# Three weight casts moved from ScalarE to VectorE, and GpSimd's decay broadcasts and key products given an order, in a two-layer hybrid encoder

## The chip, the cores and the metric

The kernel runs on one core of a Trainium2 chip. The metric is the device time of one execution in microseconds; the median of several is compared. The engines are PE (TensorE), DVE (VectorE), ACT (ScalarE), POOL (GpSimd) and SP (SyncE, which here only issues DMAs). Each works through its own instructions in order and waits on semaphores for the others.

## The reference

Two pre-norm layers on a sequence of 256 positions and width 1024, all in float32. Each layer projects the normalised input once, feeds a chunked gated DeltaNet (forward and backward) and a differential softmax attention, projects both branches, merges them with sigmoid gates and projects the result. Cut to what matters here:

```python
def chunk_gated_delta(q, k, v, g, beta):            # chunks of 64 positions, 8 heads
    g = jnp.cumsum(g.reshape(bsz, nh, nc, CHUNK), axis=-1)
    gdiff = g[..., :, None] - g[..., None, :]
    decay = jnp.where(lower, jnp.exp(jnp.where(lower, gdiff, 0.0)), 0.0)
    L = jnp.where(strict, jnp.einsum('bhncd,bhnmd->bhncm', kb, k) * decay, 0.0)
    T = lax.linalg.triangular_solve(eye + L, ..., lower=True, unit_diagonal=True)
    ...
    state = (state * jnp.exp(g_last)[..., None, None]
             + jnp.einsum('bhcd,bhce->bhde', k_c * jnp.exp(g_last[..., None] - g_c)[..., None], v_new))
...
for l in range(DEPTH):                               # DEPTH = 2
    h = rmsnorm(x, norm_w[l]); proj = h @ w_in[l]
    o_a = gated_delta_branch(...)                    # q, k, v, z of the first branch: qa, ka, va, za
    o_b = diff_attention_branch(...)                 # q, k, v, z of the second: qb, kb, vb, zb
    x = x + (sigmoid(ga) * (o_a @ w_pa[l]) + sigmoid(gb) * (o_b @ w_pb[l])) @ w_out[l]
```

The kernel uses chunks of 128 positions, two per sequence.

## The kernel before, in words

**Weights.** Every projection runs over four pairs of 128 input channels. A pair's float32 weights (`raw`, 128 partitions x 1024, 512 KB) come by a DMA on SP's queue into one of three buffers. ACT makes the rounded high part (`hi`, L230, a CAST), DVE the rest (`lo` = `raw` - `hi`, L232), and PE multiplies hi by hi, lo by hi and hi by lo. Names carry the projection, the layer and the group, and the pair: `hi_q{l}13` is pair 3 of the second q group of layer l. `proj_fm` (L298 to L302, `pf_q`) serves the convolved q, k and v, `proj_tm` (L244 to L246, `pp_qk` and others) the attention's q and k and the gates.

**Decays.** `decays(g, c)` handles four heads g of a chunk c: a DMA on POOL's queue broadcasts their cumulated log decays into `B` (L618), POOL adds for the factor of k (`kds`, L621) and masks with `affine_select` (L624), ACT takes eight Exps per call, 32 in all (L628). `weigh_k` subtracts and multiplies on DVE (`dsum` L634, `A` L635) with the gram products `kk` of PE (L611).

**The triangular solve.** `turn_blocks` takes the 32x32 blocks of `A` through memory (`adr`) into `la` and `lt`, DVE solves them in 31 steps (`X`, L670 and L671), and `spread_blocks` copies X transposed into `lt` (L674) and sends both to memory (`udr`, L678, four DMAs on POOL's queue). From there come `T` (L705, group 0 on POOL's queue, group 1 on SP's) and `U` (L709, SP). PE merges blocks with them (`y64p` L723, `zt` L737), and ACT copies y between (L727). Next on SP's queue behind U stand the weights of the gate projection, `raw_gb`. The attention heads (`sc`, maxima `mx`, Exp `es`, transposes `at`, `aT`, products `av`, and squares `sqj` of the output) run in between.

**Products of k.** `chunks` multiplies k by its factor on POOL (`ktm`, L795, four operations) and uses the result much later, in the state's matmuls `sp`.

**What sets the order.** The code is written as steps; a scheduler with a time line of its own sorts the instructions, and the program that it gives is fixed. `behind(ins)` (`tc.issue_after`) is an edge of order for that scheduler; it becomes a wait on the chip only where data ask for one. `mark` is a dictionary of instructions to point at.

Of the kernel before, what the change touches and what calls it, by code (L numbers as in the profile page):

```python
# [11 lines left out]
AF = mybir.ActivationFunctionType  # L12
# [37 lines left out]
def hybrid_encoder(  # L50
# [47 lines left out]
    def last(ap, n):  # L98
        return ap.unsqueeze(ap.ndim).to_broadcast(list(ap.shape) + [n])
# [104 lines left out]
    def behind(ins):  # L204
        return nullcontext() if ins is None else tc.issue_after(ins)

    def weights(w, c0, n, nm, homes=(None,) * 4, ahead=True, later=None, spare=(), held=None):

        for kp in range(4):
            act, dve = (later or {}).get(kp, (None, None))
            with tc.high_priority(offset=HP) if ahead and homes[kp] is None else nullcontext():
                if homes[kp] is not None:
                    hi, lo = homes[kp][:, 0], homes[kp][:, 1]
                else:
                    hi = wpool.tile([P, 2, 512], F32R, tag="hi", name=f"hi_{nm}{kp}", bufs=2)
                    lo = wpool.tile([P, 2, 512], F32R, tag="lo", name=f"lo_{nm}{kp}", bufs=2)
                if kp in spare:  # L220
                    raw = work.tile([P, 2, 512], F32, tag="w4a", name=f"raw_{nm}{kp}", bufs=2)
                else:
                    raw = wpool.tile([P, 2, 512], F32, tag="raw", name=f"raw_{nm}{kp}", bufs=3)
                load = (held or {}).get(kp)
                with behind(load):
                    (nc.scalar if load else nc.sync).dma_start(
                        out=raw[:, :, :n],
                        in_=w[kp * 256 : (kp + 1) * 256, c0 : c0 + n].rearrange("(k p) c -> p k c", p=P))
                with behind(act):
                    high = S.copy(hi[:, :, :n], raw[:, :, :n]).ins  # L230
                with behind(dve):
                    mark[nm, kp] = high, V.tensor_tensor(lo[:, :, :n], raw[:, :, :n],  # L232
                                                         hi[:, :, :n].bitcast(F32), ALU.subtract).ins
            for k in range(2):
                yield 2 * kp + k, hi[:, k, :n], lo[:, k, :n]

    def proj_tm(act, w, c0, n, evac, nm, places=(None,) * 4, spare=(), later=None):

        accs = banks2(f"pp_{nm}")
        for kt, hi, lo in weights(w, c0, n, nm, places, later=later, spare=spare):  # L240
            for m in range(NM):
                ts_ = slice(m * P, (m + 1) * P)
                o = accs[m][:, :n]
                T.matmul(o, act[kt // 4][:, 0, kt % 4, ts_], hi, start=kt == 0, stop=False)  # L244
                T.matmul(o, act[kt // 4][:, 0, kt % 4, ts_], lo, start=False, stop=False)  # L245
                mark["proj"] = T.matmul(o, act[kt // 4][:, 1, kt % 4, ts_], hi, start=False,  # L246
                                        stop=kt == KT - 1).ins
                mark["done", kt] = mark["proj"]
        for m in range(NM):
            evac(m, accs[m][:, :n])  # L250
# [33 lines left out]
            evac(m, o)  # L284
            yield

    def proj_fm(act, w, c0, evac, nm):


        accs = [a.rearrange("p (b t) -> p b t", b=2) for a in banks2(f"pf_{nm}")]  # L290
        for kt, hi, lo in weights(w, c0, 512, nm, later=mark.pop("later", None)):
            for b in range(4):
                cs = slice(b * P, (b + 1) * P)
                o = accs[b // 2][:, b % 2, :]
                first = kt == 0 and b % 2 == 0
                done = kt == KT - 1 and b % 2 == 1
                with behind(mark.pop("first", None)):
                    T.matmul(o, hi[:, cs], act[kt // 4][:, 0, kt % 4, :], start=first, stop=False,  # L298
                             skip_group_check=True)
# [41 lines left out]
    for l in range(DEPTH):  # L341
# [98 lines left out]
        def qk_part(s_, i):  # L440
                def evac_qk(m, ps):
                    st = work.tile([P, 512], F32, tag="w2a", name=f"stg{l}{s_}{i}{m}", bufs=2)
                    S.copy(st, ps)
                    g_ = st.rearrange("p (g e) -> p g e", e=DH)
                    x12 = g_[:, :, 0 : 2 * RD].rearrange("p g (x r) -> p g x r", x=2)
                    both = lambda t_: mid(mid(t_[:, m, :], 2), 8)
                    r4 = small.tile([P, 2, 8, 2, RD], F32, tag="r4", name=f"r4{l}{s_}{i}{m}", bufs=1)
                    V.tensor_tensor(r4[:, 0], x12, both(cos), ALU.mult)
                    V.tensor_tensor(r4[:, 1], x12, both(sin), ALU.mult)
                    V.tensor_tensor(x12[:, :, 0], r4[:, 0, :, 0], r4[:, 1, :, 1], ALU.subtract)  # L450
                    V.tensor_tensor(x12[:, :, 1], r4[:, 0, :, 1], r4[:, 1, :, 0], ALU.add)
# [64 lines left out]
        def conv(seg, c_base, slot, g):  # L516
            def evac_conv(acc, b0):
# [35 lines left out]
                for b in range(2):  # L553
                    for m in range(NM):
                        hd = 4 * g + b0 + b
                        S.activation(sqj[:, :P], ptv[:, b, m, :], AF.Square,
                                     accum_out=ss[:, m, hd : hd + 1])
            proj_fm(hT, wl, c_base + 512 * g, evac_conv, f"{seg}{l}{g}")

        gdr = dram.tile([NM, 8, 2, P], F32, tag="gdr", name=f"gdr{l}")  # L560
        lnc = small.tile([P, 2, NM, NH], F32, tag="lnc", name=f"lnc{l}")
# [50 lines left out]
                         start=True, stop=True)  # L612
            return heads4(gp)

        def decays(g, c):
            hs4 = slice(4 * g, 4 * g + 4)
            dec = B[:, c, hs4].rearrange("p h d i -> p d h i")
            G.dma_start(out=B[:, c, hs4].rearrange("p h d i -> p (h d i)"),  # L618
                        in_=gdr[c, hs4].rearrange("h d i -> (h d i)").partition_broadcast(P))
            end = (P - 1) * (1 - c)  # L620
            G.tensor_tensor(kds[:, c, hs4], dec[:, c, :, end], lnc[:, c, c, hs4], ALU.add)  # L621
            for d in range(2):
                sg = 1 - 2 * d
                G.affine_select(out=dec[:, d], in_=dec[:, d], compare_op=ALU.is_ge, fill=BIG,  # L624
                                base=0, pattern=[[0, 4], [sg, P]], channel_multiplier=-sg)
                for j4 in range(4):
                    h = 4 * g + j4
                    S.activation(dec[:, d, j4, :], dec[:, d, j4, :], AF.Exp,  # L628
                                 bias=lnc[:, d, c, h : h + 1])

        def weigh_k(g, c):
            dec = B[:, c, 4 * g : 4 * g + 4].rearrange("p h d i -> p d h i")
            dsum = work.tile([P, 4, P], F32, tag="w2c", name=f"dsum{l}{g}{c}", bufs=3)
            V.tensor_tensor(dsum, dec[:, 0], dec[:, 1], ALU.add)  # L634
            V.tensor_tensor(A[:, g, c], gram("kk", g, c, 0), dsum, ALU.mult)  # L635
# [37 lines left out]
        def spread_blocks():  # L673
            V.tensor_copy(lt, X.rearrange("p c i -> p i c"))  # L674
            for d in range(2):
                ps_ = slice(64 * d, 64 * d + 64)
                for w, src_ in enumerate((X, lt) if d == 0 else (lt, X)):
                    G.dma_start(out=udr[w, :, :, 8 * d : 8 * d + 8].rearrange("b g t j i -> (b g) (t j i)"),  # L678
                                in_=src_[ps_].rearrange("p j i -> p (j i)"))


        tix = lambda d, c, j4: (2 * d + c) * 4 + j4
# [92 lines left out]
        def chunks(g):  # L775
# [16 lines left out]
                S.copy(flat(y1[d]), ps)  # L792
            yield
            for d in range(2):
                G.tensor_tensor(st[d], st[d], last(kds[:, d, hs4], P), ALU.mult)  # L795
# [282 lines left out]
```

## Time and profile before

| what | value |
|---|---|
| median of 3 runs (lowest to highest) | 779.93 us (778.48 to 781.05) |
| span of the profiled execution | 777.1 us |
| the median above that span | 2.8 us |
| PE busy | 758.2 us, 98% |
| DVE busy | 557.3 us, 72% |
| ACT busy | 474.9 us, 61% |
| POOL busy | 101.9 us, 13% |
| mean granted TensorE clock | 0.996 |
| two layers of about | 378 us each |

The profiled execution has no time of its own but its span, 777.1 us from the first to the last instruction; what lies around it is taken as the 2.8 us between it and the median. In the rows of a timeline stand the start, the duration, the engine, the line, the operation, out<-in with the shape, xN for a run of N alike, and in brackets the idle time ahead and what ended it. Lines and places in layer 0 are given; layer 1 repeats them some 378 us later.

### The profile page before, as it was taken

The numbers are of one execution on the slowest core, as the hardware profiler recorded it, in microseconds if no ns is written. First come the engines' busy times: TensorE is split into PE (matmuls) and PEld (weight loads), VectorE is DVE, ScalarE is ACT, GpSimd is POOL, SyncE is SP. The second block draws the span as 40 slices with busy tenths as digits, with TensorE's granted clock in tenths as the row PEclk, the third lists the DMA queues.
The fourth block names the chain that finished last, engine by engine and source line by source line (L and its number), as shares of the span: only waits on it lengthen the run. The fifth ranks groups of instructions, "written<-read, shape, count | busy, mean of one in ns | idle before, by whom it ended". The sixth has DMA issues, their size and how long they took to land.

```text
span 777.1 us, 13805 instructions
## 1 busy us (share of the span) xinstructions
PE 758.2 (98%) x5222; PEld 647.7 (83%) x5222; DVE 557.3 (72%) x1051; ACT 474.9 (61%) x1042; POOL 101.9 (13%) x137
## 2 busy tenths in 40 slices
PE   8999999999999999999999999999999999999996
PEld 4899879887778888887889888899777788888784
DVE  5686878999974635377677776989999553536782
ACT  5657776557677744564554668655577776356551
POOL 5100461100030100010010025510001110001000
PEclk9999999999999999999999999999999999999998
DMA  7752756554496644346664256755446954343631
GB/s 227 240 177 78 224 146 198 174 172 136 112 207 187 210 135 129 117 144 210 215 224 136 82 160 221 194 170 161 141 137 174 233 164 160 114 133 111 213 110 54
DMA packets 77745, 126.91 MB, mean 163 GB/s; under 512 B 19679, under 2 KB 20015, under 8 KB 77680
## 3 DMA queue, kind: packets, MB, share of 16 engines
q1 hardware_dynamic: 71038, 112.99, 48.4%
q0 software_dynamic: 3936, 9.77, 4.8%
q10 hardware_dynamic: 2706, 3.28, 1.3%
q8 instruction: 41, 0.67, 0.4%
q14 instruction: 24, 0.20, 0.1%
HBM read 121.27 MB, written 4.75 MB: 162 GB/s over the span
## 4 chain that ended last, share of the span: by engine, by line
PE 81%; DVE 7%; DMA 5%; ACT 4%; issue 2%; POOL 0%; SPq 0%; POOLq 0%; ACTq 0%; DVEq 0%
PE pp_vb L282 5%; DMA raw_q<-in_w_in_dram 3%; PE pp_qk L245 2%; PE pp_qk L246 2%; PE pp_qk L244 2%; PE pp_o L282 2%; PE pf_k L298 2%; PE pf_k L302 2%; PE pf_v L298 2%; PE pf_k L300 2%; PE pp_gb L245 2%; PE sc L839 2%; PE pp_gb L244 2%; PE pf_v L302 2%; PE pf_v L300 2%; PE av L865 2%
## 5 line engine op out<-in xcount | busy, mean ns | idle before, releaser
L245 PE MATMUL pp_qk<-lo_qk,hT 128*128 128x512 f32 x128 | 51.3, 401 | 1.0 <-DVE lo_qk L232 1.0
L246 PE MATMUL pp_qk<-hi_qk,hT 128*128 128x512 f32 x128 | 50.1, 391 | 0.0
L230 ACT CAST hi_qk<-raw_qk 128x1024 fp32r<-128x1024 f32 x32 | 33.5, 1046 | 23.6 <-PE pp_qk L246 12.6
L244 PE MATMUL pp_qk<-hi_qk,hT 128*128 128x512 f32 x128 | 46.1, 398 | 0.7 <-ACT hi_qk L230 0.7
L232 DVE TENSOR_TENSOR lo_qk<-raw_qk,hi_qk 128x1024 fp32r<-128x1024 f32 x32 | 40.2, 1257 | 7.6 <-ACT hi_qk L230 7.4
L232 DVE TENSOR_TENSOR lo_pb<-raw_pb,hi_pb 128x1024 fp32r<-128x1024 f32 x16 | 19.6, 1224 | 35.7 <-ACT hi_pb L230 35.7
L298 PE MATMUL pf_q<-hT,hi_q 128*128 128x256 f32 x128 | 36.5, 288 | 0.3 <-ACT hi_q L230 0.2
L298 PE MATMUL pf_v<-hT,hi_v 128*128 128x256 f32 x128 | 36.5, 289 | 0.0
L300 PE MATMUL pf_v<-hT,hi_v 128*128 128x256 f32 x128 | 36.2, 286 | 0.0
L300 PE MATMUL pf_q<-hT,hi_q 128*128 128x256 f32 x128 | 35.9, 284 | 0.0
L848 ACT ACTIVATE es<-sc,mx 128x256 f32<-128x256 f32 x64 | 29.8, 473 | 10.1 <-DVE mx L846 10.0
L298 PE MATMUL pf_k<-hT,hi_k 128*128 128x256 f32 x128 | 35.8, 285 | 0.0
L302 PE MATMUL pf_q<-hT,lo_q 128*128 128x256 f32 x128 | 35.7, 292 | 0.0
L300 PE MATMUL pf_k<-hT,hi_k 128*128 128x256 f32 x128 | 35.7, 283 | 0.0
L232 DVE TENSOR_TENSOR lo_gb<-raw_gb,hi_gb 128x1024 fp32r<-128x1024 f32 x16 | 19.6, 1224 | 22.2 <-ACT hi_gb L230 22.0
L232 DVE TENSOR_TENSOR lo_ga<-raw_ga,hi_ga 128x1024 fp32r<-128x1024 f32 x16 | 19.6, 1226 | 21.0 <-ACT hi_ga L230 21.0
L302 PE MATMUL pf_v<-hT,lo_v 128*128 128x256 f32 x128 | 34.6, 286 | 0.0
L302 PE MATMUL pf_k<-hT,lo_k 128*128 128x256 f32 x128 | 34.4, 285 | 0.0
L230 ACT CAST hi_pb<-raw_pb 128x1024 fp32r<-128x1024 f32 x16 | 16.8, 1049 | 25.1 <-PE pp_pb L246 24.3
L527 DVE SCALAR_TENSOR_TENSOR cvq<-pf_q,cw,cvq 128x254 f32<-128x254 f32 (+1 forms) x64 | 29.7, 476 | 1.8 <-ACT cvq L523 1.4
L527 DVE SCALAR_TENSOR_TENSOR cvv<-pf_v,cw,cvv 128x254 f32<-128x254 f32 (+1 forms) x64 | 30.2, 483 | 0.6 <-ACT cvv L523 0.5
L527 DVE SCALAR_TENSOR_TENSOR cvk<-pf_k,cw,cvk 128x254 f32<-128x254 f32 (+1 forms) x64 | 28.5, 478 | 2.0 <-ACT cvk L523 1.3
(356 smaller groups left out, 2495.5 us busy)
## 6 DMA issues: line engine op xcount, KB each, us to landing
raw_qk<-in_w_in_dram SPq DMA_DIRECT2D x32, 512.0 KB, 3.7
raw_k<-in_w_in_dram SPq DMA_DIRECT2D x16, 512.0 KB, 4.6
raw_q<-in_w_in_dram SPq DMA_DIRECT2D x16, 512.0 KB, 3.7
raw_v<-in_w_in_dram SPq DMA_DIRECT2D x16, 512.0 KB, 3.8
raw_zb<-in_w_in_dram SPq DMA_DIRECT2D x16, 512.0 KB, 3.6
raw_za<-in_w_in_dram SPq DMA_DIRECT2D x16, 512.0 KB, 3.7
raw_gb<-in_w_in_dram SPq DMA_DIRECT2D x16, 512.0 KB, 4.7
raw_o<-in_w_out_dram SPq DMA_DIRECT2D x16, 512.0 KB, 4.5
```

Source lines behind the costliest of these rows:

```text
L230: high = S.copy(hi[:, :, :n], raw[:, :, :n]).ins
L232: mark[nm, kp] = high, V.tensor_tensor(lo[:, :, :n], raw[:, :, :n], hi[:, :, :n].bitcast(F32), ALU.subtract).ins
L244: T.matmul(o, act[kt // 4][:, 0, kt % 4, ts_], hi, start=kt == 0, stop=False)
L245: T.matmul(o, act[kt // 4][:, 0, kt % 4, ts_], lo, start=False, stop=False)
L246: mark["proj"] = T.matmul(o, act[kt // 4][:, 1, kt % 4, ts_], hi, start=False, stop=kt == KT - 1).ins
L282: mark["proj"] = T.matmul(o, a_, w_, start=kt == 0 and a_ is ah and w_ is hi, stop=kt == KT - 1 and a_ is al).ins
L298: T.matmul(o, hi[:, cs], act[kt // 4][:, 0, kt % 4, :], start=first, stop=False, skip_group_check=True)
L300: T.matmul(o, hi[:, cs], act[kt // 4][:, 1, kt % 4, :], start=False, stop=False, skip_group_check=True)
L302: T.matmul(o, lo[:, cs], act[kt // 4][:, 0, kt % 4, :], start=False, stop=done, skip_group_check=True)
L527: V.scalar_tensor_tensor(ca[:, o0:o1], acc[:, b, o0 + sft : o1 + sft], cw[:, j, cb : cb + 1], ca[:, o0:o1], ALU.mult, ALU.add)
L839: mm = T.matmul(sp[n][:, qt * SEQ : (qt + 1) * SEQ], qkT[h // 4][rows, 0, h % 4, qt * P : (qt + 1) * P], qkT[h // 4][rows, 1, h % 4, :], s ...
L848: S.activation(es[:, n, qt, :], spv[:, qt, :], AF.Exp, bias=mx[:, n, qt : qt + 1], accum_out=s_all[:, h, n, qt : qt + 1])
```

## The change

Three things, in each layer. (1) DVE instead of ACT makes the high part for pair 3 of the second q group (`hi_q{l}13`) and for pairs 0 and 1 of the attention's first k group (`hi_qk{l}010`, `hi_qk{l}011`). (2) The broadcasts of `decays(1, 0)` and `decays(1, 1)` get an edge behind the last Exps of `decays(0, 0)`. (3) The products `ktm` get an edge behind the last `udr` DMA in the code, the one from X.

```diff
-    def weights(w, c0, n, nm, homes=(None,) * 4, ahead=True, later=None, spare=(), held=None):
+    def weights(w, c0, n, nm, homes=(None,) * 4, ahead=True, later=None, spare=(), held=None, turned=()):
...
-                    high = S.copy(hi[:, :, :n], raw[:, :, :n]).ins
+                    high = (V.tensor_copy if kp in turned else S.copy)(hi[:, :, :n], raw[:, :, :n]).ins
...
-                proj_tm(hT, wl, (C_QB, C_KB)[s_] + 512 * i, 512, evac_qk, f"qk{l}{s_}{i}")
+                proj_tm(hT, wl, (C_QB, C_KB)[s_] + 512 * i, 512, evac_qk, f"qk{l}{s_}{i}",
+                        turned=(0, 1) if (s_, i) == (0, 1) else ())
...
-            proj_fm(hT, wl, c_base + 512 * g, evac_conv, f"{seg}{l}{g}")
+            proj_fm(hT, wl, c_base + 512 * g, evac_conv, f"{seg}{l}{g}",
+                    turned=(3,) if (seg, g) == ("q", 1) else ())
...
-        def decays(g, c):
+        def decays(g, c, after=None):
...
-            G.dma_start(out=B[:, c, hs4].rearrange("p h d i -> p (h d i)"),
-                        in_=gdr[c, hs4].rearrange("h d i -> (h d i)").partition_broadcast(P))
+            with behind(after):
+                G.dma_start(out=B[:, c, hs4].rearrange("p h d i -> p (h d i)"),
+                            in_=gdr[c, hs4].rearrange("h d i -> (h d i)").partition_broadcast(P))
...
-                    S.activation(dec[:, d, j4, :], dec[:, d, j4, :], AF.Exp,
-                                 bias=lnc[:, d, c, h : h + 1])
+                    mark["decay", d] = S.activation(dec[:, d, j4, :], dec[:, d, j4, :], AF.Exp,
+                                                    bias=lnc[:, d, c, h : h + 1]).ins
...
-                    G.dma_start(out=udr[w, :, :, 8 * d : 8 * d + 8].rearrange("b g t j i -> (b g) (t j i)"),
-                                in_=src_[ps_].rearrange("p j i -> p (j i)"))
+                    mark["udr"] = G.dma_start(out=udr[w, :, :, 8 * d : 8 * d + 8].rearrange("b g t j i -> (b g) (t j i)"),
+                                in_=src_[ps_].rearrange("p j i -> p (j i)")).ins
...
-                G.tensor_tensor(st[d], st[d], last(kds[:, d, hs4], P), ALU.mult)
+                with behind(mark["udr"]):
+                    G.tensor_tensor(st[d], st[d], last(kds[:, d, hs4], P), ALU.mult)
...
         decays(0, 0)
         weigh_k(0, 0)
+        seen = mark["decay", 0], mark["decay", 1]
...
-        decays(1, 0)
+        decays(1, 0, seen[0])
...
-        decays(1, 1)
+        decays(1, 1, seen[1])
```

How the scheduled programs differ is shown at three places. First POOL in layer 0, from the decays' end to the blocks; before, with the products ahead of the `adr` transfers:

```order
39 L795 TENSOR_TENSOR ktm_330<-ktm_330,kds_341 128x512 x4
40 L654 DMA adr_342<-A_339 32x16x32 x4
41 L656 DMA la_344<-adr_342 64x1024
42 L657 DMA lt_345<-adr_342 64x1024
43 L658 MEMSET X_346 128x1024
44 L659 MEMSET X_346 128x32
45 L986 TENSOR_TENSOR rq_3662<-rq_3661,mhalf 128x16
46 L678 DMA udr_343<-X_346 8x8x1024 x2
47 L678 DMA udr_343<-lt_345 8x8x1024 x2
```

And now:

```order
39 L657 DMA adr_342<-A_339 32x16x32 x4
40 L659 DMA la_344<-adr_342 64x1024
41 L660 DMA lt_345<-adr_342 64x1024
42 L661 MEMSET X_346 128x1024
43 L662 MEMSET X_346 128x32
44 L991 TENSOR_TENSOR rq_3662<-rq_3661,mhalf 128x16
45 L681 DMA udr_343<-X_346 8x8x1024 x2
46 L799 TENSOR_TENSOR ktm_330<-ktm_330,kds_341 128x512 x4
47 L681 DMA udr_343<-lt_345 8x8x1024 x2
```

The four products have moved from ahead of `adr` to between the two pairs of `udr` transfers, the edge being to the last transfer in the code, which the scheduler places second. The four broadcasts of `B`, a few rows above, stand as they did, one after the other, with the waits they had.

Second, DVE at the decays of layer 0 (`lo_q_1295` and `hi_q_1294` are pair 3 of the second q group, `qk` 1381 to 1400 the attention's first two pairs, `kk` 1103 and 1127 the grams of group 0, chunks 0 and 1, 1151 and 1175 those of group 1). Before:

```order
136 L634 TENSOR_TENSOR dsum_1101<-B_340 128x512
137 L635 TENSOR_TENSOR A_339<-kk_1103,dsum_1101 128x512
138 L232 TENSOR_TENSOR lo_q_1295<-raw_q_1296,hi_q_1294 128x1024
139 L536 SCALAR_TENSOR_TENSOR kq_329<-thq_973,cvq_967 128x2x128
140 L634 TENSOR_TENSOR dsum_1125<-B_340 128x512
141 L635 TENSOR_TENSOR A_339<-kk_1127,dsum_1125 128x512
142 L634 TENSOR_TENSOR dsum_1149<-B_340 128x512
143 L635 TENSOR_TENSOR A_339<-kk_1151,dsum_1149 128x512
144 L232 TENSOR_TENSOR lo_qk_1382<-raw_qk_1383,hi_qk_1381 128x1024
145 L634 TENSOR_TENSOR dsum_1173<-B_340 128x512
146 L635 TENSOR_TENSOR A_339<-kk_1175,dsum_1173 128x512
147 L232 TENSOR_TENSOR lo_qk_1400<-raw_qk_1401,hi_qk_1399 128x1024
```

And now:

```order
136 L230 CAST hi_q_1294<-raw_q_1296 128x1024
137 L232 TENSOR_TENSOR lo_q_1295<-raw_q_1296,hi_q_1294 128x1024
138 L637 TENSOR_TENSOR dsum_1101<-B_340 128x512
139 L537 SCALAR_TENSOR_TENSOR kq_329<-thq_973,cvq_967 128x2x128
140 L638 TENSOR_TENSOR A_339<-kk_1103,dsum_1101 128x512
141 L230 CAST hi_qk_1381<-raw_qk_1383 128x1024
142 L637 TENSOR_TENSOR dsum_1125<-B_340 128x512
143 L232 TENSOR_TENSOR lo_qk_1382<-raw_qk_1383,hi_qk_1381 128x1024
144 L637 TENSOR_TENSOR dsum_1149<-B_340 128x512
145 L638 TENSOR_TENSOR A_339<-kk_1127,dsum_1125 128x512
146 L230 CAST hi_qk_1399<-raw_qk_1401 128x1024
147 L232 TENSOR_TENSOR lo_qk_1400<-raw_qk_1401,hi_qk_1399 128x1024
```

The casts stand ahead of the decay sums, each `lo` at or near its cast, and the `A` products have slid back by a step.

Third, PE where pair 3 of the second q group begins (`hi_q_1294`, `lo_q_1295`; `kk_1127` is the gram of group 0, chunk 1). Before:

```order
458 L298 MATMUL pf_q_1202<-hT_1_108,hi_q_1294 128x256
459 L300 MATMUL pf_q_1202<-hT_1_108,hi_q_1294 128x256
460 L298 MATMUL pf_q_1203<-hT_1_108,hi_q_1294 128x256
461 L300 MATMUL pf_q_1203<-hT_1_108,hi_q_1294 128x256
462 L611 MATMUL kk_1127<-kq_329 128x128 x4
463 L302 MATMUL pf_q_1202<-hT_1_108,lo_q_1295 128x256
```

And now:

```order
458 L298 MATMUL pf_q_1202<-hT_1_108,hi_q_1294 128x256
459 L300 MATMUL pf_q_1202<-hT_1_108,hi_q_1294 128x256
460 L298 MATMUL pf_q_1203<-hT_1_108,hi_q_1294 128x256
461 L300 MATMUL pf_q_1203<-hT_1_108,hi_q_1294 128x256
462 L302 MATMUL pf_q_1202<-hT_1_108,lo_q_1295 128x256
463 L298 MATMUL pf_q_1202<-hT_1_108,hi_q_1294 128x256
```

The gram `kk_1127` has left the place between the hi and the lo matmuls and now stands at row 476, among the last of this group. Elsewhere, two of ACT's `sqj` squares ahead of the y copies now have the cast of `hi_gb` (pair 1) between them; the copy of X into `lt` and X's last step on DVE stand ahead of two maxima `mx`, a `lo_za` and a RECIPROCAL that were ahead of them; and in layer 1's tail the chunk matmuls are shuffled among the gate and output projections.

More of the change, by code (lines that the diff above doesn't have):

```diff
@@ L235, in weights, with proj_tm @@
                 yield 2 * kp + k, hi[:, k, :n], lo[:, k, :n]
-    def proj_tm(act, w, c0, n, evac, nm, places=(None,) * 4, spare=(), later=None):
+    def proj_tm(act, w, c0, n, evac, nm, places=(None,) * 4, spare=(), later=None, turned=()):
         accs = banks2(f"pp_{nm}")
-        for kt, hi, lo in weights(w, c0, n, nm, places, later=later, spare=spare):
+        for kt, hi, lo in weights(w, c0, n, nm, places, later=later, spare=spare, turned=turned):
             for m in range(NM):
@@ L285, in proj_by_tile, with proj_fm @@
             yield
-    def proj_fm(act, w, c0, evac, nm):
+    def proj_fm(act, w, c0, evac, nm, turned=()):
         accs = [a.rearrange("p (b t) -> p b t", b=2) for a in banks2(f"pf_{nm}")]
-        for kt, hi, lo in weights(w, c0, 512, nm, later=mark.pop("later", None)):
+        for kt, hi, lo in weights(w, c0, 512, nm, later=mark.pop("later", None), turned=turned):
             for b in range(4):
```

## The prediction

> **What bounds the kernel now.** I read the page first, then the waits of PE, then PE's windows at the places that the change touches, and last the engines' timelines there. The page says who sets the pace:
>
> ```profile
> PE 758.2 (98%) x5222; PEld 647.7 (83%) x5222; DVE 557.3 (72%) x1051; ACT 474.9 (61%) x1042; POOL 101.9 (13%) x137
> ```
>
> PE works 758.2 of 777.1 us. The three casts stay as much work as before and PE's matmuls stay the same in number, so an edit pays only by what it takes from PE's roughly 19 idle microseconds, and costs only by what it adds to them. The list of PE's waits (engine, line waited for, total, times, longest) shows which of those the change can touch; each came twice, once in each layer:
>
> ```profile
> PE kk L611 <- DVE A L635: 1.3, 2, 0.8
> ...
> PE pp_qk L245 <- DVE lo_qk L232: 1.0, 2, 0.5
> PE pp_zb L244 <- ACT es L848: 0.9, 2, 0.5
> ```
>
> PE's windows in layer 0 (length, then the busy time of PE, PEld, DVE, ACT, POOL, then clock, DMA share and GB/s) place them:
>
> ```profile
> 96.00:100.00 4.00, 3.77 (x32) 3.56 (x31) 1.70 (x3) 2.80 (x8) 3.13 (x7) 1.00 0.92 351
> 100.00:104.00 4.00, 3.95 (x34) 3.74 (x33) 2.43 (x4) 4.00 (x14) 2.18 (x2) 1.00 0.50 146
> 104.00:108.00 4.00, 2.96 (x18) 2.23 (x18) 3.05 (x4) 4.00 (x13) 1.73 (x2) 1.00 0.01 5
> 108.00:112.00 4.00, 3.55 (x18) 3.02 (x19) 3.42 (x5) 3.63 (x11) 4.00 (x3) 1.00 0.46 131
> 121.00:240.00 119.00, 118.48 (x817) 98.99 (x816) 106.78 (x232) 77.31 (x181) 10.38 (x15) 1.00 0.62 169
> ```
>
> In the 16 us of the decays PE misses 0.23 + 0.05 + 1.04 + 0.45 = 1.77 us, while ACT has 4.00 of 4.00 in two of the windows: there the casts queue behind the 32 Exps. In the 119 us behind, PE misses 0.52 us and DVE is at 106.78: that stretch has nothing to win and no room for a late transfer. The clock is full throughout.
>
> **The casts.** PE's four waits at the decays are these, with the gram kk001 between them:
>
> ```profile
> 99.71 0.39 PE L298 MATMUL pf_q<-hT,hi_q 128*128 128x256 f32 x1 [0.23 <-ACT hi_q L230]
> ...
> 100.29 1.06 PE L611 MATMUL kk<-kq 128*128 128x128 f32 x8
> ...
> 104.43 1.16 PE L611 MATMUL kk<-kq 128*128 128x128 f32 x8 [0.48 <-DVE A L635]
> 106.12 0.74 PE L244 MATMUL pp_qk<-hi_qk,hT 128*128 128x512 f32 x2 [0.54 <-ACT hi_qk L230]
> ...
> 108.45 0.50 PE L245 MATMUL pp_qk<-lo_qk,hT 128*128 128x512 f32 x1 [0.52 <-DVE lo_qk L232]
> ```
>
> The waits add up to the same 1.77 us. With three casts gone from ACT its Exps move up by three times 1.05, and DVE has idle time for three casts there (1.70 to 3.42 busy of 4). What they rest on, on ACT and DVE:
>
> ```profile
> 98.61 1.05 ACT L230 CAST hi_q<-raw_q 128x1024 fp32r<-128x1024 f32 x1 [1.20 <-DMA raw_q<-in_w_in_dram]
> ...
> 99.69 1.23 DVE L232 TENSOR_TENSOR lo_q<-raw_q,hi_q 128x1024 fp32r<-128x1024 f32 x1 [0.70 <-ACT hi_q L230]
> ...
> 106.63 1.76 DVE L232 TENSOR_TENSOR lo_qk<-raw_qk,hi_qk 128x1024 fp32r<-128x1024 f32 x1
> ...
> 216.15 1.12 DVE L674 COPY lt<-X 128x1024 f32<-128x1024 f32 x1
> ```
>
> No row shows a cast of this tile on DVE. The nearest is DVE's COPY of 128x1024, 1.12 us; the far end is the subtraction beside GpSimd, 1.76. Faster than 1.12 isn't excluded either: the COPY reads X turned, and a plain copy could be cheaper. I take 1.1. The Trainium skill ("VectorE: DVE Perf Modes", the perf-mode tier table) gives an fp32 copy within SBUF twice the rate of a two-input operation; an estimate from its figure would be 0.6 us, the COPY row does not show it, and by it the gain below would be near its upper end.
>
> The first cast waits for raw_q's DMA as before (that landed just ahead of 98.61), so hi_q comes at the same time and its 0.23 stays. The first lo_q matmul then comes too early: the order shows that kk001, the eight issues from 100.29, now stands behind it. PE is through the four hi matmuls at 100.29, where kk001 began; a DVE cast from about 98.55 ends at 99.65 and lo_q, 1.23 more, at 100.88: a new wait of 0.6. kk, hi_qk and lo_qk I take to wait no longer: kk001 stands some 14 matmuls further on, and each cast is placed ahead of the decay sum that waits for the next Exps. Gain at 1.1 us: 1.77 - 0.23 - 0.6 = 0.9. If the cast is quicker all four waits could go: 1.8. To this comes up to 0.45 at pp_zb, if ACT, with three casts fewer behind it, reaches the Exp es it waits for sooner. Gain per layer: 0.9 to 2.2, I take 1.5.
>
> **The broadcasts.** POOL's rows of the order show the four B transfers in the same place with no wait for an Exp: the edge only tells the scheduler an order, and it had that order already. I count nothing for it.
>
> **GpSimd's products.** They stood where POOL had nothing urgent; the order now has them between two pairs of transfers:
>
> ```profile
> 106.27 6.45 POOL L795 TENSOR_TENSOR ktm<-ktm,kds 128x512 f32<-128x512 f32 x4 [4.09 <-ACT kds L651]
> ...
> 216.71 1.25 POOL L678 DMA_DIRECT2D udr<-X  x2 [72.29 <-DVE X L671]
> 217.95 1.10 POOL L678 DMA_DIRECT2D udr<-lt  x2
> ...
> 225.15 1.96 SPq L705 DMA_DIRECT2D T<-udr  x4
> 227.21 5.78 SPq L709 DMA_DIRECT2D U__96<-udr  x4
> 233.09 7.01 SPq L226 DMA_DIRECT2D raw_gb<-in_w_in_dram  x4
> ```
>
> POOL works in order, so udr<-lt is issued 6.45 us after the X pair. Behind it wait T and, on the same SP queue, U and the weights raw_gb. At 106 the products' departure is worth only the slower lo_qk there (1.76 against 1.23), which is in the gain. The products themselves are read much later, by the sp matmuls, and are done long before.
>
> Against the 6.45 stands that X ends earlier. In the order these rows of DVE no longer stand before it:
>
> ```profile
> 213.20 0.68 DVE L846 TENSOR_REDUCE mx<-sc 128x2 f32<-128x512 f32 x1
> ...
> 213.92 1.22 DVE L232 TENSOR_TENSOR lo_za<-raw_za,hi_za 128x1024 fp32r<-128x1024 f32 x1
> 215.06 0.69 DVE L846 TENSOR_REDUCE mx<-sc 128x2 f32<-128x512 f32 x1
> ...
> 215.78 0.17 DVE L851 RECIPROCAL cc<-s_all 128x2 f32<-128x2 f32 x1
> ```
>
> They overlap a little; from 213.20 on they take up 2.2 us that X no longer waits, the sum of 0.68, 1.22, 0.69 and 0.17 less half a microsecond of overlap. So udr<-X is issued at 214.5, the products run from 215.8 to 222.2, and udr<-lt goes out at 222.2 instead of 217.95: 4.25 later. Some comes back, for the lt pair no longer shares the DMA engines with the X pair (KB each, median us to landing):
>
> ```profile
> udr<-X POOLq DMA_DIRECT2D x4, 256.0 KB, 4.4
> udr<-lt POOLq DMA_DIRECT2D x4, 256.0 KB, 6.5
> ```
>
> If lt lands as X does, 2.1 is regained; if not, none. T starts 2.15 to 4.25 later; I take 3.2. U and raw_gb follow by as much. This is how that meets PE:
>
> ```profile
> 235.68 0.31 ACT L871 ACTIVATE sqj<-ob 128x128 f32<-128x128 f32 x1
> ...
> 237.40 1.05 ACT L230 CAST hi_gb<-raw_gb 128x1024 fp32r<-128x1024 f32 x1 [1.31 <-DMA raw_gb<-in_w_in_dram]
> 238.35 0.64 ACT L727 COPY y<-y64p 128x256 f32<-128x256 f32 x2
> 238.88 0.60 ACT L861 COPY aT<-at 128x512 f32<-128x512 f32 x1
> ...
> 239.53 1.16 PE L865 MATMUL av<-vb,aT 128*128 128x128 f32 x8
> ```
>
> ACT is in order too. It already waits 1.31 us for raw_gb; the casts, then y and aT follow one upon another; aT ends at 239.48 and av starts at 239.53. There is no slack: what raw_gb loses, PE loses at av. Moreover the square sqj (0.31, some 0.4 with its readout) now stands behind hi_gb instead of before it. Stall per layer: 3.2 + 0.4 = 3.6, from 2.5 (lt as quick as X, 2.15 + 0.4) to 4.7. In layer 1 the cast ends its wait just as its load arrives, so I take the same:
>
> ```profile
> 614.75 1.04 ACT L230 CAST hi_gb<-raw_gb 128x1024 fp32r<-128x1024 f32 x1 [0.58 <-PE pp_za L246]
> ```
>
> The y64p matmuls and zt need T and U, later by the same 3.2 and behind the same stall. The order also shuffles the tail of layer 1 (chunk matmuls between the projections); with PE idle there for about a microsecond at most now, I cost it at zero, bounds -1 and +1.
>
> **The sum.** Per layer 3.6 - 1.5 = +2.1, twice: +4.2 on the profiled 777.1 us gives a span of 781.3. The median of 779.93 lies 2.8 above the span; added alike that is 784.1, and I say 784. Ends of this case: least stall with most gain, 2 x (2.5 - 2.2) - 1 = -0.4; most stall with least gain, 2 x (4.7 - 0.9) + 1 = +8.6. So 779.5 to 788.5 by itself.
>
> **The rivals.**
>
> *The lateness finds cover, only the decays count* (faster). It decides at raw_gb: if its first load starts less than 1.5 us later than now, a layer gains on balance. For it: U's issues take 5.78 us in layer 0, a queue that is full of earlier transfers; a later start may meet an emptier one. Against it: the hi_gb row waits for the DMA already. With no stall at all: 2 x -1.5 = -3, 776.9.
>
> *Much the same.* The two terms cancel, near the lower end of my own case: 779.9, give or take 2.3, which is 0.3% and about what a measurement of this kernel can tell from no change.
>
> *The broadcasts do move, so the change does what it says.* Then raw_q, which loads beside four transfers of 512 KB, would come sooner than these rows show:
>
> ```profile
> 86.71 2.18 POOL L618 DMA_DIRECT2D B<-gdr  x4 [1.84 <-ACT E L597]
> ...
> raw_q<-in_w_in_dram SPq DMA_DIRECT2D x16, 512.0 KB, 3.7
> ```
>
> hi_q's 0.23 and the new 0.6 at lo_q go, 0.8 a layer: 784.1 - 1.6 = 782.5. Against it speaks the order; I give 3%, within the slower side.
>
> *DVE and GpSimd get in each other's way* (slower still). The lo_qk beside the products took 1.76 against 1.23, the row of lo_q: 0.53 more. The first cast lies beside affine_selects of B, of which the second pair, beside lo_q's subtraction, took twice as long as the first:
>
> ```profile
> 98.19 1.22 POOL L624 TENSOR_SCALAR_AFFINE_SELECT B<-B 128x512 f32<-128x512 f32 x2
> ...
> 99.70 2.48 POOL L624 TENSOR_SCALAR_AFFINE_SELECT B<-B 128x512 f32<-128x512 f32 x2
> ```
>
> If the cast must wait out one affine_select of the first pair, hi_q is 0.6 later and the gain of 0.9 sinks to 0.3; and the products now run beside DVE at 216 to 222, where it is nearly full, and slow some three large operations there by 0.53 each: 1.6, of which I let half reach PE by way of the scores' maxima. A layer: 3.6 - 0.3 + 0.8 = +4.1, in all +8.2: 788. It decides from the point where DVE's slowdown beside POOL is more than PE's slack there, which the 119-us window puts near none. The Trainium skill ("SBUF — State Buffer", Reading the diagram and the box on SWDGE) says that a DVE fp32 copy within SBUF can lock GpSimd out of a shared pair of ports for the whole instruction; the 1.76 and the 2.48 are a slowdown of such a kind, but beside two-input operations, and no row here shows a DVE copy beside POOL.
>
> **How the numbers follow.** My case 0.5 and the contention 0.1 make slower 0.6, with the 3% in it. The covered lateness has 0.27: it asks for one mistaken link of a long chain. The same has 0.13. The likeliest is 784. The range starts at 776.5, just under the covered case, and ends at 788.5, the upper end of mine.
>
> **What would show it.** In the changed profile: three CASTs (one hi_q, two hi_qk) on DVE of about 1.1 us; PE's four waits at the decays replaced by about 0.6 at pf_q L302 and 0.2 at L298; udr<-lt on POOL right behind a ktm of about 6.5 us; SP's T some 3 us later against PE's pp_za; a wait of 3 to 4 us at av, hi_gb's wait for raw_gb grown alike. It is wrong if av waits for nothing, or if the casts take less than 0.8 or more than 1.5 us.

## The result, and the profile after

The changed kernel takes 783.89 us (median; 783.23 to 784.17) against 779.2 us for the kernel before in the same runs: 1.0058 times as long, 95% interval 1.0046 to 1.0071. Its profiled execution spans 781.3 us, 4.2 more than before, which is the forecast to a tenth. The profile shows that the time got there mostly by another way than the forecast's.

The page of the changed kernel has the same work on PE, and 12 us more on DVE than the 557.3 of before; six casts of under 1 us, three a layer, cannot be all of that:

```profile
PE 758.5 (97%) x5222; PEld 649.6 (83%) x5222; DVE 569.1 (73%) x1057; ACT 470.0 (60%) x1036; POOL 95.2 (12%) x137
```

PE's waits say where it was held up (engine, line, releaser: total, times, longest). The av wait that was forecast isn't there; a wait for lo_za, which the kernel before didn't have, leads the list:

```profile
PE pp_za L245 <- DVE lo_za L232: 3.8, 2, 1.9
...
PE pf_q L302 <- DVE lo_q L232: 1.2, 2, 0.6
PE pp_zb L244 <- ACT es L852: 0.9, 2, 0.4
PE pf_q L298 <- DVE hi_q L230: 0.8, 1, 0.8
PE pp_za L244 <- DVE za L313: 0.7, 1, 0.7
PE ctq L545 <- DVE kq L537: 0.7, 2, 0.4
```

The windows of layer 0 that answer to those of before (PE 3.77, 3.95, 2.96, 3.55 and 118.48) show the gain and the loss:

```profile
96.00:100.00 4.00, 3.94 (x34) 3.73 (x33) 1.24 (x2) 4.00 (x15) 2.71 (x7) 1.00 0.91 351
100.00:104.00 4.00, 3.05 (x24) 2.64 (x23) 4.00 (x6) 4.00 (x16) 2.46 (x2) 1.00 0.48 140
104.00:108.00 4.00, 4.00 (x24) 3.29 (x24) 3.90 (x6) 2.68 (x12) 0.00 (x0) 1.00 0.27 58
108.00:112.00 4.00, 4.00 (x24) 3.44 (x23) 3.96 (x7) 1.35 (x4) 0.00 (x0) 1.00 0.68 211
121.00:240.00 119.00, 115.96 (x793) 96.72 (x792) 107.95 (x223) 73.85 (x174) 14.93 (x21) 1.00 0.62 164
```

At the decays PE now misses 0.06 + 0.95 = 1.01 us instead of 1.77, and from 121 to 240 it misses 3.04 instead of 0.52. PE's first matmul of some stages dates both:

| stage | before, us | after, us | difference |
|---|---|---|---|
| layer 0, pf_v (behind the decays) | 121.0 | 120.0 | -1.0 |
| layer 0, pp_za | 205.4 | 204.2 | -1.2 |
| layer 0, pp_pb | 278.5 | 280.2 | +1.7 |
| layer 1, pf_v | 499.1 | 500.7 | +1.6 |
| layer 1, pp_za | 583.5 | 584.9 | +1.4 |
| last pp_o | 768.9 | 773.1 | +4.2 |

Up to pp_za, layer 0 gains 1.2 us, 1.0 of it by the end of the decays, and layer 1 gains 0.3 (from +1.7 to +1.4). Behind pp_za, layer 0 loses 2.9 by its next gate, pp_pb; layer 1, where the order of the tail has changed, loses 2.8 by the end. DVE, POOL and PE at that place in layer 0:

```profile
213.14 0.69 DVE L850 TENSOR_REDUCE mx<-sc 128x2 f32<-128x512 f32 x1
213.74 5.32 DVE L232 TENSOR_TENSOR lo_za<-raw_za,hi_za 128x1024 fp32r<-128x1024 f32 x1
```

```profile
212.65 1.26 POOL L681 DMA_DIRECT2D udr<-X  x2 [71.95 <-DVE X L674]
213.93 4.04 POOL L799 TENSOR_TENSOR ktm<-ktm,kds 128x512 f32<-128x512 f32 x4
217.92 1.16 POOL L681 DMA_DIRECT2D udr<-lt  x2
```

```profile
219.12 0.50 PE L245 MATMUL pp_za<-lo_za,hT 128*128 128x512 f32 x1 [1.87 <-DVE lo_za L232]
```

A subtraction that took 1.22 in the kernel before (at 213.92) lasts 5.32: by its row it begins just before the products, and ends 1.1 us behind the last of them (217.97), as if it had started only then. In layer 1 another lo_za lasts 5.32 beside the products, which run from 594.65 to 598.68. Behind it the maxima, the Exps and za are 3 to 4 us late too; PE loses 1.87 at once and another 0.73 at za.

The transfers that were to be late hardly are. udr<-lt is issued at 217.92 where it was 217.95, and SP's queue has raw_gb at 232.77 where it was 233.09. PE is 1.2 us ahead by then, so against PE udr<-lt comes about 1 us later, where 4.25 was forecast:

```profile
226.31 1.93 SPq L708 DMA_DIRECT2D T<-udr  x4
228.34 4.33 SPq L712 DMA_DIRECT2D U__96<-udr  x4
232.77 8.99 SPq L226 DMA_DIRECT2D raw_gb<-in_w_in_dram  x4
```

### The profile page after: what moved, and what is told of

It reads as the page before. It is cut to its first block, busy times and chain, and to the rows that moved or that the text cites. A ratio compares the mean times of both kernels' runs of the same rounds, so it can differ in the third digit from the quotient of the medians.

```text
span 781.3 us, 13797 instructions
## 1 busy us (share of the span) xinstructions
PE 758.5 (97%) x5222; PEld 649.6 (83%) x5222; DVE 569.1 (73%) x1057; ACT 470.0 (60%) x1036; POOL 95.2 (12%) x137
## 4 chain that ended last, share of the span: by engine, by line
PE 75%; DVE 13%; DMA 5%; ACT 3%; issue 2%; POOL 0%; SPq 0%; POOLq 0%; DVEq 0%; ACTq 0%
PE pp_vb L282 5%; DMA raw_q<-in_w_in_dram 3%; PE pp_qk L245 2%; PE pp_qk L244 2%; PE pp_qk L246 2%; DVE lo_za L232 2%; PE pp_o L282 2%; PE pf_v L298 2%; PE pf_v L302 2%; PE pp_gb L245 2%; PE pp_gb L246 2%; DMA raw_vb<-in_w_in_dram 2%; PE pp_gb L244 2%; PE pf_v L300 2%; PE pp_pb L245 2%
## 5 line engine op out<-in xcount | busy, mean ns | idle before, releaser
L230 ACT CAST hi_qk<-raw_qk 128x1024 fp32r<-128x1024 f32 x28 | 29.3, 1048 | 26.5 <-PE pp_qk L246 15.7
L232 DVE TENSOR_TENSOR lo_za<-raw_za,hi_za 128x1024 fp32r<-128x1024 f32 x16 | 27.7, 1733 | 4.7 <-ACT hi_za L230 4.4
L245 PE MATMUL pp_za<-lo_za,hT 128*128 128x512 f32 x64 | 26.4, 412 | 3.8 <-DVE lo_za L232 3.8
```

The source lines that it names most:

```text
L230: high = (V.tensor_copy if kp in turned else S.copy)(hi[:, :, :n], raw[:, :, :n]).ins
```

## The experiments

Two theories went into them. **Lock**: DVE operations that read two tensors of SBUF cannot run beside GpSimd's products. **Queue**, the prediction's: the products make udr<-lt late, and T, U, raw_gb and the matmuls behind them. All kernels are the changed kernel with the edit shown, or one named before; a ratio is to the kernel before in the same runs.

### The casts without the edge on the products

```diff
-                with behind(mark["udr"]):
-                    G.tensor_tensor(st[d], st[d], last(kds[:, d, hs4], P), ALU.mult)
+                G.tensor_tensor(st[d], st[d], last(kds[:, d, hs4], P), ALU.mult)
```

> The changed kernel without the edge on the products: they go back to their old place beside the decays, the three casts stay on VectorE. Two theories of where the changed kernel loses its 2.9 us per layer. Lock: VectorE's two-input subtraction lo_za stands still while GpSimd's products run (5.32 us where 1.22 is usual) and PE waits for it. Queue (the prediction's): the udr transfers behind the products, and T, U and raw_gb behind these, come late. Both expect only the casts' gain to be left, as the first layers of the two traces give it (1.2 us in layer 0, 0.3 in layer 1): 1.5 us less than the kernel before, 777.7 us, and no lo_za above 1.3 us.

783.02 us, 1.0033 (1.0017 to 1.0050): slower than before, where both theories expected it faster. The products now stand beside the casts, and it costs DVE and POOL both:

```profile
104.41 1.29 DVE L230 CAST hi_qk<-raw_qk 128x1024 fp32r<-128x1024 f32 x1
105.62 1.52 DVE L637 TENSOR_TENSOR dsum<-B 128x512 f32<-128x512 f32 x1
107.07 2.06 DVE L232 TENSOR_TENSOR lo_qk<-raw_qk,hi_qk 128x1024 fp32r<-128x1024 f32 x1
```

```profile
104.11 5.92 POOL L798 TENSOR_TENSOR ktm<-ktm,kds 128x512 f32<-128x512 f32 x4 [0.50 <-ACT kds L654]
```

In the changed kernel the same three take 0.68, 0.68 and 1.21, and the products 4.04. So the edge on the products did protect the casts; PE's waits at lo_qk come to 3.1 us in this kernel, both layers together. The expectation failed because it had looked for the lock only at lo_za.

### The edge on the products alone

```diff
-                        turned=(0, 1) if (s_, i) == (0, 1) else ())
+                        turned=())
...
-                    turned=(3,) if (seg, g) == ("q", 1) else ())
+                    turned=())
```

> The kernel before with only the edge on the products, all casts on ScalarE. Both theories expect it slower: the lock by 2.9 + 2.8 = 5.7 us (785 us) with one VectorE operation of some 5 us beside the products in each layer and a wait of PE for it; the queue by 7.2 us (786 us, the prediction's 3.6 a layer) with the wait at av and at hi_gb's load.

787.24 us, 1.0090 (1.0062 to 1.0117). The stall is there without any cast; this time a pair of es products (0.88 elsewhere) is caught, no lo_za:

```profile
217.13 5.26 DVE L860 SCALAR_TENSOR_TENSOR es<-es,cc 128x256 f32<-128x256 f32 x2
```

```profile
217.67 4.03 POOL L799 TENSOR_TENSOR ktm<-ktm,kds 128x512 f32<-128x512 f32 x4
```

The interval, 785.0 to 789.3 us, fits both theories; the rows fit the lock. PE waits at `at` for es (3.3 us) and at pp_za for za (2.6), and nowhere at av or for raw_gb.

### The products behind all four transfers

```diff
-                    mark["udr"] = G.dma_start(out=udr[w, ...
+                    sent = G.dma_start(out=udr[w, ...
+                    if src_ is lt:
+                        mark["udr"] = sent
```

> The changed kernel with the edge to the last udr<-lt transfer, so that the products stand behind all four udr transfers and none of these waits for them. Queue: T, U and raw_gb are early again, the loss goes, 777.7 us. Lock: the products still run beside the same VectorE operations, only 1.2 us later; a two-input operation beside them takes some 4 us more and the time stays at 783 to 784 us.

779.31 us, 0.9992 (0.9975 to 1.0009): the loss goes, as the queue theory had it; the lock theory had 783 to 784 and missed. The rows show how the lock can be there all the same:

```profile
214.74 0.67 DVE L852 TENSOR_REDUCE mx<-sc 128x2 f32<-128x512 f32 x1
215.34 0.14 DVE L857 RECIPROCAL cc<-s_all 128x2 f32<-128x2 f32 x1
216.50 2.44 DVE L858 SCALAR_TENSOR_TENSOR cc<-s_all,neglam,cc 128x2 f32<-128x2 f32 x1 [1.02 <-ACT es L854]
```

```profile
214.88 4.04 POOL L801 TENSOR_TENSOR ktm<-ktm,kds 128x512 f32<-128x512 f32 x4
```

Beside the products DVE now has a maximum of a PSUM tile, a RECIPROCAL and 1.02 us of idleness, all of them unharmed, and then cc, two numbers a partition, which takes 2.44 instead of 0.22 and ends with the products. DVE's stall is 2.2 instead of 4.1 us and falls on a place with more slack: PE waits 0.4 us a layer for za. This run doesn't tell the theories apart; fills_for_products does.

### The products on VectorE

```diff
-                with behind(mark["udr"]):
-                    G.tensor_tensor(st[d], st[d], last(kds[:, d, hs4], P), ALU.mult)
+                with behind(mark["mix"]):
+                    V.tensor_tensor(st[d], st[d], last(kds[:, d, hs4], P), ALU.mult)
```

`mark["mix"]` is the last head's product of es (L860).

> The changed kernel with the four products on VectorE, behind the last head's mixing of its two softmaxes, where VectorE idles 3.9 us (242.9 to 247.6 in the profile of before); GpSimd has none. Both theories expect no stall: 777.7 us with the casts' gain alone, 0.5 less if the products' old place beside the decays also slowed VectorE (lo_qk 1.76 against 1.23).

777.85 us, 0.9968 (0.9951 to 0.9984), as expected. With the casts back on ScalarE:

> The kernel products_on_dve with all casts on ScalarE again: what the three casts are worth when GpSimd has no products. Casts' gain as read from PE's times in the changed kernel (1.2 and 0.3 us): this one slower than products_on_dve by 1.5 us, 779.3. If instead the products' leaving the decays made all the difference (lo_qk 1.76 against 1.23): the same as products_on_dve, 777.9.

778.47 us, 0.9986 (0.9975 to 0.9997). By the ratios the casts are worth 0.0018, about 1.4 us; the intervals overlap, so this pair doesn't prove it.

### The transfers late, without the products

To products_on_dve, eight memsets between the two pairs of transfers (`send(w, d, tile)` issues one of the four):

```diff
+            sent = [send(0, 0, X), send(1, 1, X)][1]
+            for _ in range(8):
+                with behind(sent):
+                    sent = G.memset(fill, 0.0).ins
+            for w, d in ((1, 0), (0, 1)):
+                with behind(sent):
+                    send(w, d, lt)
```

> The kernel products_on_dve with eight memsets of a spare 128x512 tile between the udr<-X and the udr<-lt transfers (some 4 us in all, as the products alone took 4.04): they delay the same transfers and read nothing. Queue (the prediction's): udr<-lt 4 us later, T and raw_gb 2 to 4 later, PE waits at av, 2 to 4.4 us a layer, so 782 to 786 us. Lock: no VectorE operation is stretched; the transfers' lateness finds slack since X ends 4 us sooner than before, 777.9 us.

776.75 us, 0.9959 (0.9943 to 0.9975): no loss. The memsets hold udr<-lt back by 4.6 us, more than the products did, to 219.03, while lo_za beside them keeps its 1.22:

```profile
214.46 4.62 POOL L686 MEMSET fill<- 128x512 f32 x8
219.03 1.10 POOL L681 DMA_DIRECT2D udr<-lt  x2
```

```profile
214.29 1.22 DVE L233 TENSOR_TENSOR lo_za<-raw_za,hi_za 128x1024 fp32r<-128x1024 f32 x1
```

From the first matmul of pp_za to udr<-lt it takes 14.2 us here, 13.7 in the changed kernel and 12.6 in the kernel before. So the lateness that the changed kernel has, and half a microsecond more, costs nothing, and the queue theory doesn't explain its loss. Whether the 4.25 of the forecast would have cost something, no run shows. What is left is that the products read SBUF while DVE does, which memsets don't; the next run tests that.

### The lock by itself

A small kernel has five kinds of VectorE operations, four of each in turn (subtraction of two SBUF tiles; cast; maxima of a PSUM tile; maxima of an SBUF tile; product of a PSUM and an SBUF tile).

> None of the network is computed, so the whole time says nothing: a small kernel with only VectorE operations of five kinds (4 each) on 128 partitions, each alone and then beside GpSimd's four products of 128x512 as they are in the kernel, ScalarE starting both. Lock: the two-input subtraction from SBUF (1.14 us apart alone) waits for products: four of them take 4.6 us alone and 8 to 9 us beside the four products, and one that comes while products are queued takes up to 5.3; the cast (0.6 apart alone) waits too, as in casts_only; the maxima of a PSUM tile, the one-input maxima of an SBUF tile and the product with one input in PSUM keep their times. Rival, shared bandwidth: every operation that reads SBUF, one input or two, is slower by the same share beside the products, and none waits for a whole product.

DVE's rows, the five kinds alone and then beside four products:

```profile
8.73 5.00 DVE L108 TENSOR_TENSOR lo<-raw,hi 128x1024 f32<-128x1024 f32 x4 [0.72 <-ACT hi L108]
14.45 2.88 DVE L108 CAST cast<-hi 128x1024 fp32r<-128x1024 f32 x4 [0.72 <-ACT hi L108]
17.87 2.87 DVE L108 TENSOR_REDUCE m<-sc 128x2 f32<-128x512 f32 x4 [0.54 <-ACT sc L108]
21.20 2.85 DVE L108 TENSOR_REDUCE m<-hi 128x2 f32<-128x512 f32 x4 [0.47 <-ACT hi L108]
24.52 2.87 DVE L108 TENSOR_TENSOR lo<-sc,hi 128x512 f32<-128x512 f32 x4 [0.47 <-ACT hi L108]
33.55 7.62 DVE L108 TENSOR_TENSOR lo<-raw,hi 128x1024 f32<-128x1024 f32 x4 [6.16 <-ACT hi L108]
42.33 5.49 DVE L108 CAST cast<-hi 128x1024 fp32r<-128x1024 f32 x4 [1.16 <-ACT hi L108]
48.79 2.87 DVE L108 TENSOR_REDUCE m<-sc 128x2 f32<-128x512 f32 x4 [0.97 <-ACT sc L108]
53.78 2.85 DVE L108 TENSOR_REDUCE m<-hi 128x2 f32<-128x512 f32 x4 [2.13 <-ACT hi L108]
58.63 2.87 DVE L108 TENSOR_TENSOR lo<-sc,hi 128x512 f32<-128x512 f32 x4 [2.01 <-ACT hi L108]
```

And POOL's, alone, beside the subtractions, beside the casts:

```profile
28.26 4.03 POOL L108 TENSOR_TENSOR kt<-kt,kd 128x512 f32<-128x512 f32 x4 [27.81 <-ACT kd L108]
33.12 6.98 POOL L108 TENSOR_TENSOR kt<-kt,kd 128x512 f32<-128x512 f32 x4 [0.83 <-ACT z L108]
41.89 5.37 POOL L108 TENSOR_TENSOR kt<-kt,kd 128x512 f32<-128x512 f32 x4 [1.80 <-ACT z L108]
```

The subtractions go from 5.00 to 7.62 us and the casts from 2.88 to 5.49, and the products from 4.03 to 6.98 and 5.37; the other three kinds and the products beside them (4.03 each) don't change by 0.03. A shared bandwidth is an unlikely cause: the one-input maxima read SBUF too and don't slow at all. The Trainium skill ("SBUF — State Buffer", section "SBUF: two separate sides") calls it an exclusive lock on a pair of ports, between a GpSimd operation and a DVE operation in a two-port mode or, where the GpSimd operation reads SBUF, one with two SBUF inputs; whichever starts first has the pair for the whole instruction. This run agrees in which kinds suffer, and the memsets above, which read nothing, do no harm.

The engines take turns here, each waiting for one operation of the other: beside the subtractions the products begin 2.0 us apart, alone 1.0. One subtraction that waits out four products is not in this run.

### What makes it wait for all four

> None of the network is computed. In lock_alone VectorE and GpSimd took turns, one operation each (a subtraction beside products 1.5 to 1.9 us apart), while in the changed kernel one subtraction waited out all four products (5.32). What differs there: GpSimd issues two transfers right before the products. The same products and subtractions as in lock_alone, with two transfers or with two memsets right ahead of the products, and maxima of a PSUM tile ahead of the subtractions. If the transfers matter: a subtraction of 4 to 5.3 us only in the sections with transfers. If it matters that the first product has no wait of its own on its engine: also in the sections with memsets. If neither: turns everywhere, and the cause of the long wait stays open.

With two transfers issued right ahead of the products, a subtraction that begins 0.3 us behind the first product waits for all of them:

```profile
35.16 1.22 DVE L112 TENSOR_TENSOR lo<-raw,hi 128x1024 f32<-128x1024 f32 x1
36.30 0.68 DVE L112 TENSOR_REDUCE m<-sc 128x2 f32<-128x512 f32 x1
36.90 4.80 DVE L112 TENSOR_TENSOR lo<-raw,hi 128x1024 f32<-128x1024 f32 x1
```

```profile
35.44 1.12 POOL L112 DMA_DIRECT2D dr<-other  x2 [0.25 <-issue]
36.58 4.03 POOL L112 TENSOR_TENSOR kt<-kt,kd 128x512 f32<-128x512 f32 x4
```

In all three sections with transfers the products keep their 4.03 and DVE gets no turn, in the first section not even for a subtraction whose row begins 0.1 us ahead of the first product; in the three with memsets in their place, turns as before (products 6.98 to 7.84). That fits the products at 106 us in the kernel before (6.45 with turns, no transfer ahead of them) and those at 214 in the changed one, where the row of lo_za too begins 0.19 us ahead of the products. Why a transfer issued by GpSimd does this, no run shows.

### The broadcasts really held back

The edge on the broadcasts, (2) of the change, left them where they were: POOL issues the four within 2.18 us, from 86.83 on, where it was 86.71 before. Here ACT issues the second pair, and with that they move. First on products_on_dve:

```diff
-                G.dma_start(out=B[:, c, hs4].rearrange("p h d i -> p (h d i)"),
+                (nc.scalar if after else G).dma_start(out=B[:, c, hs4].rearrange("p h d i -> p (h d i)"),
```

> The kernel products_on_dve with the second group's two broadcasts issued from ScalarE's queue behind the last Exps of the first, so that they do come later, as the change meant. If raw_q's load beside the four broadcasts is what holds the first VectorE cast (PE waits 0.9 at L298 and 1.2 at L302 in products_on_dve): raw_q lands sooner and 0.8 us a layer is won, 776.2 us. If the later broadcasts hold the second group's Exps and its products A instead: PE waits at kk or kq for 2 to 4 us a layer, 781 to 785 us.

772.72 us, 0.9908 (0.9892 to 0.9924): the fastest kernel of all, 6.7 us below the kernel before. PE, which misses 1.01 us of these 16 in the changed kernel, misses none:

```profile
96.00:100.00 4.00, 4.00 (x37) 4.00 (x36) 3.86 (x6) 4.00 (x15) 2.28 (x4) 1.00 0.77 254
100.00:104.00 4.00, 4.00 (x36) 4.00 (x36) 4.00 (x5) 3.44 (x12) 2.13 (x4) 1.00 0.92 319
104.00:108.00 4.00, 4.00 (x25) 3.51 (x25) 3.64 (x6) 3.74 (x16) 1.26 (x3) 1.00 0.54 158
108.00:112.00 4.00, 4.00 (x24) 3.44 (x23) 3.94 (x7) 2.04 (x6) 0.00 (x0) 1.00 0.45 131
```

The second pair goes out at 95.03 and 96.53, 6.8 and 8.3 us behind the first pair's start at 88.19. That is later, but not behind the Exps: the row of Exps starts at 95.38. The slowest load of raw_q takes 7.4 us from issue to landing in each layer, where it was 10.6 and 11.4 in products_on_dve; the cast of hi_q comes at 96.85 without a wait, where it was 98.66 in the changed kernel after 3.35 us of waiting for the load:

```profile
96.85 0.94 DVE L230 CAST hi_q<-raw_q 128x1024 fp32r<-128x1024 f32 x1
```

The later broadcasts cost nothing: PE's list has no wait for kk or kq. The gain over products_on_dve is 5.1 by the medians and 4.7 by the ratios, three times what was expected (1.6). It lies between the first pf_q and the first pf_v, here for layer 0 in products_on_dve and then in broadcasts_held:

```profile
63.10:119.80 56.70, 55.68 (x375) 49.96 (x374) 45.27 (x84) 41.70 (x114) 16.77 (x23) 1.00 0.58 172
```

```profile
64.70:119.40 54.70, 54.70 (x375) 49.87 (x375) 46.11 (x85) 41.85 (x114) 15.50 (x21) 1.00 0.59 179
```

This stretch is 2.0 us shorter; in layer 1 it goes from 57.5 to 54.7, 2.8 shorter. PE's idle time there, 1.0 and 1.8, makes up only part of that: the same 375 matmuls are also busy for 1.0 us less. A matmul of pf_q lasts 0.28 while the next begins 0.12 us behind it, so they overlap, and a stop probably costs PE more than the idle time that the list shows.

The edit changes two things, when the second pair goes out and whose queue carries it; no run tells them apart. Without the casts:

> The kernel broadcasts_held with all casts on ScalarE: what the three casts are worth once the broadcasts are held. If they are worth what they were without the hold (778.47 less 777.85): 773.3 us. If the hold alone does it: 772.7 us. If the casts are what lets the Exps finish in time there (ScalarE is full, 4.00 of 4.00 at 100 to 108): 775 us or more.

777.52 us, 0.9967 (0.9955 to 0.9979). So neither does it alone. Against dve_products_no_casts (0.9986) the casts without the hold give 0.0018, the hold without the casts 0.0019, and both 0.0078, 6 us. Without the casts PE waits for A and lo_qk again (0.8 and 0.7 us); without the hold for the load of raw_q. The same line in the changed kernel itself:

> The changed kernel as it is, but with the second group's broadcasts on ScalarE's queue, so that they do come later. The lock at the products stays (5.3 us at a two-input operation, 2.8 us of PE a layer), the waits at the decays go as in broadcasts_held: 783.9 less 5.1 (777.85 to 772.72), 778.8 us. If the held broadcasts instead need VectorE's products to pay: 782 to 784 us.

779.99 us, 1.0003 (0.9987 to 1.0019): 4 us better than the change as it was made, though no faster than the kernel before (778.8 was expected), and with the lock still there:

```profile
PE pp_za L245 <- DVE lo_za L232: 3.7, 2, 1.9
```

## Why the prediction was right, and where it wasn't

The time was right, and partly by luck: the terms were -3.0 and +7.2, and -1.5 and +5.7 were measured. Two errors of 1.5 us cancel in the sum of +4.2. That the products would cost more than the casts bring was right; how they cost it was not, and by the prediction's own signs two steps failed: av waits for nothing, and four of the six casts take 0.68 us, under its 0.8.

- **The decays, -1.5 a layer.** Measured -1.2 and -0.3. The new wait at the first lo_q, 0.6 by the working, is 0.59 in each layer, and the waits at kk, hi_qk and lo_qk are gone. The cast was mis-sized: 0.68 us for hi_qk, 0.94 and 0.91 for hi_q beside the affine_selects, not 1.1. The estimate of 0.6 from the tier table of the Trainium skill ("VectorE: DVE Perf Modes") was nearer than the row of the turned COPY. Layer 1 was taken to be as layer 0, but its waits before were others: 0.8 at kk, 0.5 and 0.2 at lo_qk and hi_qk, none for hi_q. Now it waits 0.76 for hi_q, whose load came late, 0.59 for lo_q, and 0.36 at ctq, whose kq took 0.85 us beside an affine_select where it had taken 0.51; so little is won there. The 0.45 at pp_zb stayed.
- **The products, +3.6 a layer.** Measured +2.9 and +2.8, but at lo_za and za, not at av. The step that failed is the path: the working let the products act on PE by way of udr<-lt, U and raw_gb, and they act through DVE, whose lo_za stands still for their 4.04 us. The links of the forecast's own path were mis-sized as well. The products took 4.04, not 6.45 (the 6.45 held DVE's turns, which the working read as POOL's own time). X ended at 212.07, 4.05 us sooner than before, where 2.2 was foreseen; another 1.2 is the gain at the decays, which the working left out of this chain, and for the remaining 0.65 no run shows a cause. U's issues took 4.33, not 5.78. So udr<-lt came only about 1 us later against PE, and fills_for_products shows that this costs nothing. For layer 1 the row at 614.75 names a wait for PE's pp_za and not for the load, so it was no ground for taking the same stall there.
- **The fourth rival**, DVE and GpSimd in each other's way, had the mechanism at 216 to 222, at a chance of 0.1, with its sign right and its size wrong: three operations slowed by 0.53 each, half of it reaching PE, where one operation lost 4.1 and PE 2.9.
- **The broadcasts.** That they would not move was right. What their moving would be worth was put at 1.6 us for both layers; with the lock out of the way and the casts on DVE it was about 5, where they were moved to ACT's queue as well.
- **The tail of layer 1** was put at nothing; between pp_za and the end layer 1 loses 2.8, no more than layer 0 loses at its stall, 2.9.

## What to carry to other kernels

A sum that comes out right doesn't show that its terms are right: look in the changed profile for the wait that the forecast named. The time of an operation in a trace can hold another engine's turns: compare it with the same operation where the other engine is idle before moving it by that time. Before giving GpSimd an elementwise operation on SBUF, look at what VectorE does beside it: subtractions and casts of SBUF tiles pay for it, work from PSUM and maxima of one SBUF tile don't, and right behind a transfer that GpSimd issues the price here was the whole run of its four operations. An order edge between two engines is worth a look in the scheduled program, for here it moved nothing. Issuing two of the four broadcasts later and from another queue was worth about 6 us together with the casts, and each of the two alone about 1.4, which these runs don't set clearly apart from nothing.

## What the hardware showed that wasn't expected

- Four products of GpSimd right behind two transfers of its own queue let no two-input VectorE operation in for 4.03 us; without the transfers, or with memsets instead, the engines alternate after each operation, and beside subtractions the four products last 6.0 to 7.8 us.
- An operation on 128x2 waits like a large one: cc took 2.44 us instead of 0.22 beside the products.
- A 512 KB load beside four broadcasts of 512 KB landed 10.6 us after its issue and kept its cast waiting 3.35 us; with two of the four issued later, from ACT's queue, the slowest took 7.4 and the cast waited for nothing.
